# Weight sums for two projections: from accumulating DMAs to VectorE, in pieces, during the attention

## The chip, the core and the metric

The kernel runs on one core of a Trainium2 chip. Its time is the device time of one execution in microseconds; before the change the median of three runs is 1688.66 us (1685.91 to 1690.49). The core has TensorE (PE, matrix products), VectorE (DVE), ScalarE (ACT), GpSimd (POOL) and SyncE (SP). SyncE only issues transfers. GpSimd issues transfers too, among them the accumulating ones (the transfer adds to what stands at its destination). All transfers run on the same 16 DMA engines.

## What is computed

The reference is two layers of a decoder trunk on 512 positions of width 2048, all in float32. The even layer projects x into a gated short convolution and into a sparse attention of 8 heads, gates both, and projects back (`w_out`, 2048 x 2048). The odd layer is a gated MLP:

```python
def odd_layer(x, w_in, ln_g, ln_b, sgu_w, sgu_b, w_out):
    h = x @ w_in
    uv = jax.nn.gelu(h[..., :2 * D_SGU])
    z = h[..., 2 * D_SGU:]
    u, v = jnp.split(uv, 2, axis=-1)
    v = layer_norm(v, ln_g, ln_b)...
    mixed = jnp.einsum('gts,bnsgc->bntgc', w_causal, v) + sgu_b...
    y = u * mixed.reshape(bsz, s, D_SGU) * jax.nn.silu(z)
    return y @ w_out
```

After each layer stands a LayerNorm of the residual. The projections that matter here are those for u and z (2048 x 4096 together), for v, and the two output projections.

## The kernel before

A float32 operand is split into a high half (`hi`, rounded to float32r) and a low half (`lo`, the rest). ScalarE makes `hi` (L85), VectorE makes `lo` (L86), and every product is three matmuls. Weights come as raw pages of 128x1024 (512 KB) on SyncE's queue; there are four raw pages, and four pairs of `hi` and `lo` pages in the pool `wp`.

The stages follow each other: first the projections and the attention, head by head (the loop over h, six column units of 48 matmuls in each head and the head's scores, softmax and products); then five passes, each one Strassen-like product (`strassen`): the output projection of the even layer (wo0), v, u/z in two passes r = 0 and 1 (u and z share a pass: block column g of the pass belongs to half of u and z), and the last output projection (wo1). Strassen's scheme replaces eight block products by seven, numbered 1, 2, 5, 3, 6, 7, 4 in their order; each product p takes a block, or a sum of blocks, of the weights and of the activations. One product has two halves c of the inner dimension; for each half the activation piece is split (`shi`, `slo`) and then the weights of two block columns g are used by two row tiles m: 48 matmuls of 128x512 per (p, c), 14 of them per pass.

The sums of weight blocks come in two ways. In wo0, v and wo1 (`chained`, L613) pages x in SBUF are kept and GpSimd accumulates the next block into them; only sum 7 is made ahead, in DRAM. In the u/z passes (`plain`) all four sums 5, 7, 6, 4 are made ahead in DRAM by `weight_sums`. One step of it is four tiles of 512 KB: GpSimd writes one element of `after` into each tile (L227; this only makes the step wait for `after`), copies a block or an earlier sum into it (L232) and accumulates a second block (L238). There are 8 steps for each r and 2 for each of the three other sums. `early`, 16 steps, runs in the attention, two per head: wo0's, v's, all of r = 0 and the first four of r = 1. `late`, the other four of r = 1, and `steps1` (wo1's two) run in the passes: two steps of `late` in v (L817, L822), two in u/z r = 0, `steps1` in u/z r = 1 (L945, L949). A pass loads the ready sums as raw pages (L585).

In the u/z passes SyncE's queue also carries the rows of the LayerNorm (L874) and a residual chain: load `xs` (L898), two VectorE operations (L899, L900), store to `xres` (L901), with two buffers.

Engines run their instructions in a fixed order each. The framework that builds the program puts them in that order: what is ready first by its own estimate goes first, and among the ready ones the earlier in the text. Waits are semaphores; an engine whose next instruction waits does nothing else.

Of the kernel before, what the change touches and what calls it, by code (L numbers as in the profile page):

```python
# [65 lines left out]
def trunk(ctx, tc, xT, xn, oneh, cst, table, wa, wv, convw, posT, cw1, cw2, wo0, wuz, wv1, odg, odb, sguw, sgub, wo1, out):  # L66
# [24 lines left out]
    def load_unit(src, n, cut=1024):  # L91

        parts = []
        for c in range(0, n, cut):
            w = min(cut, n - c)
            raw = raw_page()
            nc.sync.dma_start(raw[:, :w], src[:, c:c + w])
            hi = wp.tile([P, 1024], F32R, tag="hi", name="whi", bufs=4)
            lo = wp.tile([P, 1024], F32R, tag="lo", name="wlo", bufs=4)
            split(hi[:, :w], lo[:, :w], raw[:, :w])  # L100
            parts.append((hi, lo))
        return parts
# [38 lines left out]
    for half in range(2):  # L141
        ws = {}
        for u in range(2):
            ws[u] = (wp.tile([P, 1024], F32R, tag="hi", name="whi", bufs=4), wp.tile([P, 1024], F32R, tag="lo", name="wlo", bufs=4))
        for i, (k0, k1) in enumerate(XCH[half]):
            for u, w0, w1 in WCH[half][i]:
                nc.sync.dma_start(wraw[u][half][:, w0:w1], wa[u][:, half * 1024 + w0:half * 1024 + w1])
            nc.sync.dma_start(xraw[:, k0:k1, :], xT[:, k0:k1, :])
        for i, (k0, k1) in enumerate(XCH[half]):
            for u, w0, w1 in WCH[half][i]:  # L150
                split(ws[u][0][:, w0:w1], ws[u][1][:, w0:w1], wraw[u][half][:, w0:w1])
            split(act_hi[:, k0:k1, :], act_lo[:, k0:k1, :], xraw[:, k0:k1, :])
        for k0, k1 in XCH[half]:
            for u in range(2):
                hi, lo = ws[u]
                for kt in range(k0, k1):
# [85 lines left out]
    sums0, steps0 = weight_sums(blocks(wo0), (7,), "ts0_")  # L242
    sumsv, stepsv = weight_sums(blocks(wv1), (7,), "tsv_")
    sums1, steps1 = weight_sums(blocks(wo1), (7,), "ts1_")
    sumsu, stepsu = zip(*(weight_sums(uz_blocks(r), (5, 7, 6, 4), f"tu{r}_") for r in range(2)))
    early = steps0 + stepsv + stepsu[0] + stepsu[1][:4]
    late = stepsu[1][4:]


    with ExitStack() as es:  # L250
# [229 lines left out]
        for h in range(NH):  # L480
            bh = ap.tile([P, BW], F32, name="bh")
            skew = rscr[h].rearrange("p r -> (p r)")[P - 1:P - 1 + P * (RLEN - 1)].rearrange("(p r) -> p r", r=RLEN - 1)[:, 0:BW]
            nc.sync.dma_start(bh, skew)
            bc = ap.tile([P, NT, NCMP], F32, name="bc")
            nc.gpsimd.memset(bc, NEG)
            for qb in range(NT):
                n = 8 * qb + 7
                j0 = BW - P + CB - 1 - P * qb
                nc.gpsimd.tensor_copy(bc[:, qb, :n], bh[:, j0:j0 + CS * (n - 1) + 1:CS])
            ps = next_a()  # L490
            qT = ap.tile([P, S], F32, name="qT", bufs=1)
            nc.scalar.activation(qT, ps, AF.Copy, scale=QSCALE)  # L492
            q_hi = ap.tile([P, S], F32R, name="q_hi", bufs=1)
            q_lo = ap.tile([P, S], F32R, name="q_lo", bufs=1)
            split(q_hi, q_lo, qT)
            q = qT, q_hi, q_lo
            if h == 0:
                cmp_half(1, 1)
                cmp_hidden(1)
            ps = next_a()  # L500
            if h == 0:
                cmp_out(1)
            bz = silu2(ps, "bz")
            for copies, _ in early[2 * h:2 * h + 2]:
                copies(qT[0:1, 0:1])
            t0, tc_ = softmax_branch(h, 0, q, bh, bc)
            compressed(h, tc_)

            ps = next_a()
            ah = ap.tile([P, S], F32, name="ah", bufs=1)  # L510
            nc.scalar.copy(ah, ps)
            transpose_c(tc_)
            p0 = transpose_p(t0)
            for _, adds in early[2 * h:2 * h + 2]:
                adds()
            ps = next_a()
            t1, _ = softmax_branch(h, 1, q, bh)
            u = ap.tile([P, S + 2], F32, name="u", bufs=1)
            nc.vector.memset(u[:, 0:2], 0.0)
            nc.vector.tensor_tensor(u[:, 2:], ps, ah, ALU.mult)  # L520
            nc.vector.tensor_scalar(ah, u[:, 0:S], convT[:, h, 0:1], None, ALU.mult)
            for k in (1, 2):
                nc.vector.scalar_tensor_tensor(ah, u[:, k:k + S], convT[:, h, k:k + 1], ah, ALU.mult, ALU.add)
            po = bank("po")
            products3(po, vc_hi[:, h // HPG], vc_lo[:, h // HPG], pc_hi, pc_lo, True, False)
            values_product(po, 0, p0)
            ps = next_a()
            nc.vector.tensor_tensor(ah, ps, ah, ALU.mult)
            p1 = transpose_p(t1)
            ps = next_a()  # L530
            az = silu2(ps, "az")
            nc.vector.scalar_tensor_tensor(y_sb[:, h, :], ah, YSCALE, az, ALU.mult, ALU.mult)  # L532
            values_product(po, 1, p1)
            nc.vector.scalar_tensor_tensor(y_sb[:, 8 + h, :], bz, YSCALE, po, ALU.mult, ALU.mult)
            if h == HPG - 1:
                key_unit(0)
                key_unit(1)
                values_and_gates(1)
                compressed_keys(1)
# [48 lines left out]
    def plain(get, sums):  # L588

        def unit(p, g, c, d):  # L590
            return raw_load(sums[p, g, c, d] if p in (5, 7, 6, 4) else get(*{1: (0, 0), 2: (1, 0), 3: (1, 1)}[p], g, c, d))
        return unit

    def chained(get, sums, pool, direct):
# [19 lines left out]
            return x[g, c, d]  # L614
        return unit

    def strassen(sp, src, unit, done, more=2, by_tile=False, wx=None, cuts=False):

# [15 lines left out]
        def weights(p, g, c):  # L634
            parts = []
            for d in range(2):
                raw = unit(p, g, c, d)
                pool = wx if wx and count[0] % 3 == 2 else wp
                count[0] += 1
                hi = pool.tile([P, 1024], F32R, tag="hi", name="whi", bufs=2 if pool is wx else 4)  # L640
                lo = pool.tile([P, 1024], F32R, tag="lo", name="wlo", bufs=2 if pool is wx else 4)
                split(hi, lo, raw)
                parts.append((hi, lo))
            return parts
# [107 lines left out]
    ex_ = ExitStack()  # L752
    ex = ex_.enter_context(tc.tile_pool(name="ex", bufs=1, side="right"))
    exq = ex.tile([P, 3, 2, 4, 256], F32, name="exq")
    xc_ = ExitStack()
    xc = xc_.enter_context(tc.tile_pool(name="xc", bufs=1))
    xhat = [dram.tile([P, DM], F32, name=f"xhat{m}") for m in range(NT)]
# [37 lines left out]
        if p == 5:  # L795
            nc.sync.dma_start(xv[:, 2 + m, cols(g, 0)], xn[(2 + m) * P:(3 + m) * P, cols(g, 0)])

    strassen(sp, in_place(quarters(y_sb)), chained(blocks(wo0), sums0, xc, (0,)), prefill)


    uv = {}
# [1 line left out]
    def done_v(p, g, m, b):  # L803
# [11 lines left out]
        elif p == 5:  # L815
            nc.scalar.copy(v(1, 1), b)
            if m:  # L817
                late[g][0](v(1, 1)[0:1, 0:1])
        elif p == 3:
            nc.scalar.copy(v(0, 1), b)  # L820
            if m:
                late[g][1]()  # L822
        elif p == 6:
            add(uv[g, m], b)

# [25 lines left out]
        return {1: xq(0, 0, c), 2: xq(0, 1, c), 5: xq(1, 0, c), 3: sd(c), 7: s3(c), 6: z(c), 4: xq(1, 1, c)}[p]  # L851

    made = []
    strassen(sp, x_sums, chained(blocks(wv1), sumsv, xc, (0,)), done_v)
    drain(len(later))
    mom = [moments(statsv, m, EPS) for m in range(NT)]
    xc_.close()
# [5 lines left out]
    with tc.tile_pool(name="sgu", bufs=2) as sg:  # L863
# [48 lines left out]
        def uz_done(r):  # L912
# [24 lines left out]
            def done(p, g, m, b):  # L937
# [3 lines left out]
                elif p == 2:  # L941
                    u[0, g, m] = tile()
                    nc.scalar.activation(u[0, g, m], b, AF.Gelu_apprx_tanh)
                    if m:
                        (late[2:], steps1)[r][g][0](u[0, g, m][0:1, 0:1])  # L945
                    if r == 1 and (g, m) == (1, 1):
                        later.extend(lambda mt=mt, q=q: y_turn(mt, q) for q in range(2) for mt in range(NT))
                elif p == 5:
                    if m:  # L949
                        (late[2:], steps1)[r][g][1]()  # L950
                    z[1, g, m] = tile()
                    nc.scalar.copy(z[1, g, m], b)
                elif p == 3:
# [20 lines left out]
        for r in range(2):  # L974
            for q in (2 * r, 2 * r + 1):
                values(q)
            for q in (2 * r, 2 * r + 1):
                residual_rows(q)
            strassen(sp, x_sums, plain(uz_blocks(r), sumsu[r]), uz_done(r), cuts=True)
        while later:  # L980
            drain(1)
    ex_.close()


    with tc.tile_pool(name="fin", bufs=1) as fin, tc.tile_pool(name="wx", bufs=1, side="right") as wx:
# [35 lines left out]
        strassen(sp, in_place(yT), chained(blocks(wo1), sums1, fin, (0,)), take1, by_tile=True, wx=wx)  # L1021


# [84 lines left out]
```

## Time and profile before

| | |
|---|---|
| median of 3 runs | 1688.66 us (1685.91 to 1690.49) |
| profiled execution | 1688.4 us, span 1686.6 us |
| mean granted TensorE clock | 0.973 |
| busy: TensorE, VectorE, ScalarE, GpSimd | 1597.9, 968.0, 685.8, 315.1 us |
| attention (with the first projections) | up to about 777 us |
| wo0, v | about 777 to 935, 935 to 1100 us |
| u/z r = 0, r = 1 | about 1100 to 1298, 1298 to 1485 us |
| wo1 and the end | about 1485 to 1687 us |

Times in the trace count from the start of the span. "Busy" is the time in which an engine executes; the granted clock is the share of TensorE's full clock (1 is 2.4 GHz). The time to landing of a transfer runs from its issue to its last byte.

### The profile page before, as it was taken

The page shows a single profiled execution, that of the slowest core. Times are in us where ns is not written, and L with a number is a line of the kernel's source. Part 1 is how long each engine was busy: PE and PEld are TensorE (multiplying, and loading weights), DVE is VectorE, ACT ScalarE, POOL GpSimd, SP SyncE. Part 2 cuts the span into 40 slices and gives each one's busy share as a digit, 9 for nine tenths or more (in the row PEclk, how much of TensorE's full clock was granted, in tenths as well). Part 3 has the DMA queues.
Part 4 walks back from the last instruction along what each step waited for, and adds up shares of the span by engine and source line. Part 5 has one row for each costly group of instructions (what it writes and reads, how often), then busy time and mean ns, then how long its engine had stood idle before and what let it go on. Part 6 is the DMA issues. An engine that isn't in the chain of part 4 may idle for free.

```text
span 1686.6 us, 19659 instructions
## 1 busy us (share of the span) xinstructions
PE 1597.9 (95%) x7333; PEld 1321.9 (78%) x7333; DVE 968.0 (57%) x1438; ACT 685.8 (41%) x965; POOL 315.1 (19%) x429
## 2 busy tenths in 40 slices
PE   8899999999999999999899999997699998999995
PEld 6698888888888888887688888775477886877784
DVE  5224453534244444455559875885389744974688
ACT  4123232323233323234355765552344554555441
POOL 0104041312021404041131214103100040011311
PEclk9899999999999999999999999998899999999898
DMA  5549696969259688699999979959966799579962
GB/s 208 195 138 258 147 237 145 248 165 236 84 175 219 187 182 215 149 248 251 225 226 241 276 194 273 246 176 292 259 212 197 241 277 250 170 241 280 225 158 81
DMA packets 157243, 355.34 MB, mean 211 GB/s; under 512 B 15227, under 2 KB 85683, under 8 KB 155868
## 3 DMA queue, kind: packets, MB, share of 16 engines
q0 software_dynamic: 72896, 139.00, 40.3%
q1 hardware_dynamic: 84108, 214.68, 38.3%
q8 instruction: 57, 0.93, 0.2%
q10 hardware_dynamic: 144, 0.41, 0.1%
q14 instruction: 38, 0.31, 0.1%
HBM read 341.42 MB, written 107.52 MB: 266 GB/s over the span
## 4 chain that ended last, share of the span: by engine, by line
PE 74%; DMA 13%; DVE 6%; issue 5%; ACT 1%; POOL 1%; SPq 0%; DVEq 0%; POOLq 0%; ACTq 0%
PE ps L111 12%; PE ps L113 12%; PE ps L112 12%; PE ps L664 9%; PE ps L665 9%; PE ps L663 9%; DMA raw<-in_wuz_dram 3%; DVE wlo L86 2%; DMA x<-in_wo_dram 2%; DMA row<-odrow 2%; PE ps_t L436 1%; DMA xs<-xhat 1%; DMA xv<-xres 1%; PE ps L122 1%; PE ps L120 1%
## 5 line engine op out<-in xcount | busy, mean ns | idle before, releaser
L86 DVE TENSOR_TENSOR wlo<-raw,whi 128x1024 fp32r<-128x1024 f32 (+2 forms) x322 | 385.3, 1203 | 452.8 <-ACT whi L85 447.4
L85 ACT CAST whi<-raw 128x1024 fp32r<-128x1024 f32 (+2 forms) x322 | 333.5, 1036 | 756.2 <-PE ps L112 312.6
L664 PE MATMUL ps<-wlo,shi 128*128 128x512 f32 x1120 | 450.6, 402 | 40.0 <-DVE wlo L86 39.8
L663 PE MATMUL ps<-whi,shi 128*128 128x512 f32 x1120 | 448.8, 404 | 16.2 <-ACT whi L85 15.5
L665 PE MATMUL ps<-whi,slo 128*128 128x512 f32 x1120 | 447.1, 400 | 1.3 <-DVE slo L86 1.3
L111 PE MATMUL ps<-act_hi,whi 128*128 128x512 f32 x864 | 340.4, 394 | 4.0 <-ACT whi L85 4.0
L113 PE MATMUL ps<-act_hi,wlo 128*128 128x512 f32 x864 | 337.6, 391 | 0.0
L112 PE MATMUL ps<-act_lo,whi 128*128 128x512 f32 x864 | 337.4, 390 | 0.0
L664 PEld LDWEIGHTS ps<-wlo,shi 128*128 128x128 f32 x1120 | 216.9, 194 | 96.4 <-DVE wlo L86 51.0
L663 PEld LDWEIGHTS ps<-whi,shi 128*128 128x128 f32 x1120 | 216.6, 193 | 67.9 <-ACT whi L85 20.5
L665 PEld LDWEIGHTS ps<-whi,slo 128*128 128x128 f32 x1120 | 216.4, 193 | 47.8 <-DVE slo L86 2.0
L111 PEld LDWEIGHTS ps<-act_hi,whi 128*128 128x128 f32 x864 | 163.0, 189 | 36.8 <-ACT whi L85 4.3
L113 PEld LDWEIGHTS ps<-act_hi,wlo 128*128 128x128 f32 x864 | 162.7, 188 | 35.0 <-DVE wlo L86 0.8
L112 PEld LDWEIGHTS ps<-act_lo,whi 128*128 128x128 f32 x864 | 162.9, 189 | 32.4
L86 DVE TENSOR_TENSOR wlo<-x,whi 128x1024 fp32r<-128x1024 f32 x84 | 101.7, 1219 | 40.9 <-ACT whi L85 40.3
L85 ACT CAST whi<-x 128x1024 fp32r<-128x1024 f32 x84 | 87.9, 1050 | 72.8 <-PE ps L665 61.7
L613 POOL DMA_DIRECT2D x<-in_wo_dram x48 | 42.6, 943 | 252.3 <-DMA x<-in_wo_dram 166.5
L238 POOL DMA_DIRECT2D tu<-in_wuz_dram x64 | 76.9, 2142 | 19.0 <-DMA tu<-tu 13.3
L227 POOL DMA_DIRECT2D tu<-qT x48 | 26.1, 603 | 251.7 <-ACT qT L492 251.7
L86 DVE TENSOR_TENSOR slo<-y_sb,shi 128x1024 fp32r<-128x1024 f32 x52 | 63.3, 1217 | 0.2 <-ACT shi L85 0.2
L85 ACT CAST shi<-y_sb 128x1024 fp32r<-128x1024 f32 x52 | 54.6, 1051 | 3.9 <-DVE y_sb L532 1.7
L417 ACT ACTIVATE t_sc<-t_sc,mx 128x128 f32<-128x128 f32 (+1 forms) x64 | 35.2, 551 | 17.2 <-DVE mx L414 17.1
(212 smaller groups left out, 1454.9 us busy)
## 6 DMA issues: line engine op xcount, KB each, us to landing
raw<-in_wa_dram SPq DMA_DIRECT2D x110, 512.0 KB, 5.4
tu<-in_wuz_dram POOLq DMA_DIRECT2D x96, 512.0 KB, 17.4
raw<-tu SPq DMA_DIRECT2D x64, 512.0 KB, 4.5
x<-in_wo_dram POOLq DMA_DIRECT2D x48, 512.0 KB, 10.0
raw<-in_wuz_dram SPq DMA_DIRECT2D x48, 512.0 KB, 5.7
raw<-in_wo_dram SPq DMA_DIRECT2D x40, 512.0 KB, 8.0
ts<-in_wo_dram POOLq DMA_DIRECT2D x32, 512.0 KB, 12.4
tu<-tu POOLq DMA_DIRECT2D x32, 512.0 KB, 8.4
```

Of the source, the lines that this page charges most:

```text
L85: nc.scalar.copy(hi, src)
L86: nc.vector.tensor_tensor(lo, src, hi.bitcast(F32), ALU.subtract)
L111: nc.tensor.matmul(ps, hi[:, w], act_hi[:, kt, :], start=kt == 0, stop=False)
L112: nc.tensor.matmul(ps, hi[:, w], act_lo[:, kt, :], start=False, stop=False)
L113: nc.tensor.matmul(ps, lo[:, w], act_hi[:, kt, :], start=False, stop=kt == KT - 1)
L227: nc.gpsimd.dma_start(h[0:1, 0:1], after)
L238: nc.gpsimd.dma_start(same(t[q, g, c, d], src), src, accum_op=ALU.add, max_dma_last_dim=1024)
L417: nc.scalar.activation(t[:, offs[qb]:offs[qb] + nk], t[:, offs[qb]:offs[qb] + nk], AF.Exp, bias=mx[:, qb:qb + 1], accum_out=sm[:, qb:qb + 1])
L613: nc.gpsimd.dma_start(x[g, c, d], get(*{5: (0, 1), 6: (1, 1), 4: (1, 0)}[p], g, c, d), accum_op=ALU.add)
L663: nc.tensor.matmul(o, s[0][:, k, ms], moving(hi, k), start=new and c == 0 and k == 0, stop=False, **kw)
L664: nc.tensor.matmul(o, s[0][:, k, ms], moving(lo, k), start=False, stop=False, **kw)
L665: nc.tensor.matmul(o, s[1][:, k, ms], moving(hi, k), start=False, stop=c == 1 and k == 3, **kw)
```

## The change

The four sums of the u/z weights are no longer made by accumulating DMAs. An item (r, g, c, i) loads four tiles of 128x512 (256 KB each, in runs of 2 KB) on SyncE's queue, adds four times on VectorE, in place, and stores each of the four as one sum on GpSimd's queue (runs of 1 KB). The tiles have four buffers in the attention's pool (`wsum`). There are 32 items, four per head, in the text at four places of the head loop. `early` keeps four steps, one for each of the first four heads. `steps1` moves into the v pass, to the place of the two steps of `late`; no step is left in the u/z passes.

The four buffers take the space of one `hi`/`lo` pair: `wp` has three pairs instead of four. The passes get the missing one from a pool `wx`: 3 + 1 pairs in wo0, v and u/z, 3 + 3 (before 4 + 2) in wo1, taken in turn.

```diff
-            hi = wp.tile([P, 1024], F32R, tag="hi", name="whi", bufs=4)
-            lo = wp.tile([P, 1024], F32R, tag="lo", name="wlo", bufs=4)
+            hi = wp.tile([P, 1024], F32R, tag="hi", name="whi", bufs=3)
+            lo = wp.tile([P, 1024], F32R, tag="lo", name="wlo", bufs=3)
...
-    sumsu, stepsu = zip(*(weight_sums(uz_blocks(r), (5, 7, 6, 4), f"tu{r}_") for r in range(2)))
-    early = steps0 + stepsv + stepsu[0] + stepsu[1][:4]
-    late = stepsu[1][4:]
+    early = steps0 + stepsv
+    sumsu = [{(q, g, c): dram.tile([P, 2, 4, 256], F32, name=f"tu{r}_{q}{g}{c}") for q in (5, 7, 6, 4) for g, c in GCS} for r in range(2)]
+
+    def uz_sums(pool, r, g, c, i):
+
+        q = 2 * r + g
+
+        def load(k, n):
+            t = pool.tile([P, 512], F32, tag="wsum", name="wsum", bufs=4)
+            nc.sync.dma_start(t, wuz[8 * q + 2 * i + n][:, (2 * k + c) * 512:(2 * k + c + 1) * 512])
+            return t
+
+        def add_store(p, t, o):
+            nc.vector.tensor_tensor(t, t, o, ALU.add)
+            nc.gpsimd.dma_start(sumsu[r][p, g, c][:, :, i], t.rearrange("p (d e) -> p d e", d=2))
+        b12, b22, b11, b21 = load(0, 1), load(1, 1), load(0, 0), load(1, 0)
+        add_store(7, b22, b12)
+        add_store(5, b12, b11)
+        add_store(6, b11, b22)
+        add_store(4, b21, b11)
+
+    uz_items = iter([(r, g, c, i) for r in range(2) for g, c in GCS for i in range(4)])
...
-            for copies, _ in early[2 * h:2 * h + 2]:
+            for copies, _ in early[h:h + 1]:
                 copies(qT[0:1, 0:1])
             t0, tc_ = softmax_branch(h, 0, q, bh, bc)
             compressed(h, tc_)
+            uz_sums(ap, *next(uz_items))
...
-            return raw_load(sums[p, g, c, d] if p in (5, 7, 6, 4) else get(*{1: (0, 0), 2: (1, 0), 3: (1, 1)}[p], g, c, d))
+            return raw_load(sums[p, g, c][:, d] if p in (5, 7, 6, 4) else get(*{1: (0, 0), 2: (1, 0), 3: (1, 1)}[p], g, c, d))
...
-                pool = wx if wx and count[0] % 3 == 2 else wp
+                pool, bufs = (wx, nx) if count[0] % (3 + nx) >= 3 else (wp, 3)
...
             if m:
-                late[g][0](v(1, 1)[0:1, 0:1])
+                steps1[g][0](v(1, 1)[0:1, 0:1])
...
-                    if m:
-                        (late[2:], steps1)[r][g][0](u[0, g, m][0:1, 0:1])
...
-                    if m:
-                        (late[2:], steps1)[r][g][1]()
```

## Rows read from the trace of the kernel before

**Rows 1.** Page, busy microseconds (share of the span), instructions.
```profile
PE 1597.9 (95%) x7333; PEld 1321.9 (78%) x7333; DVE 968.0 (57%) x1438; ACT 685.8 (41%) x965; POOL 315.1 (19%) x429
```

**Rows 2.** Busy time by stretch: engines, then granted clock, DMA share, GB/s.
```profile
60.00:777.00 717.00, 715.53 (x3576) 610.57 (x3577) 300.14 (x652) 218.54 (x423) 161.19 (x238) 1.00 0.75 193
1100.00:1298.00 198.00, 168.30 (x669) 132.24 (x668) 140.75 (x171) 84.61 (x97) 19.90 (x26) 0.91 0.79 229
1298.00:1485.00 187.00, 180.21 (x798) 147.41 (x797) 124.38 (x140) 97.77 (x116) 18.56 (x24) 0.98 0.80 235
```

**Rows 3.** TensorE's waits, 60 to 777 us: total, times, longest us.
```profile
PE ps L111 <- ACT whi L85: 4.0, 1, 4.0
...
```

**Rows 4.** TensorE's waits, 1100 to 1298 us.
```profile
PE ps L664 <- DVE wlo L86: 21.3, 9, 6.7
PE ps L663 <- ACT whi L85: 8.1, 5, 2.8
```

**Rows 5.** ScalarE in order of time, casts of activation pieces in the u/z passes.
```profile
1099.90 1.06 ACT L85 CAST shi<-y_sb 128x1024 fp32r<-128x1024 f32 x1
...
1163.30 1.04 ACT L85 CAST shi<-y_sb 128x1024 fp32r<-128x1024 f32 x1
...
1239.53 1.06 ACT L85 CAST shi<-exq 128x1024 fp32r<-128x1024 f32 x1
...
1302.72 1.06 ACT L85 CAST shi<-y_sb 128x1024 fp32r<-128x1024 f32 x1
...
1360.60 1.06 ACT L85 CAST shi<-y_sb 128x1024 fp32r<-128x1024 f32 x1
```

**Rows 6.** Chain that ended last, 1300 to 1330 us: start, us, what.
```profile
1308.35 1.73 PE pm L929 x8
...
```

**Rows 7.** GpSimd in order of time, u/z r = 0: first and last lines of 24 transfers.
```profile
1153.46 2.17 POOL L227 DMA_DIRECT2D tu<-uz  x4 [35.15 <-ACT uz L943]
...
1187.86 1.14 POOL L238 DMA_DIRECT2D tu<-in_wuz_dram  x1 [0.28 <-DMA tu<-tu]
```

**Rows 8.** Transfers issued from 1160 to 1225 us: count, KB, median us to landing.
```profile
raw<-in_wuz_dram SPq DMA_DIRECT2D x8, 512.0 KB, 14.7
raw<-tu SPq DMA_DIRECT2D x5, 512.0 KB, 13.6
```

**Rows 9.** Transfers issued from 1230 to 1290 us.
```profile
raw<-tu SPq DMA_DIRECT2D x19, 512.0 KB, 4.5
...
```

**Rows 10.** Busy time by stretch in u/z r = 1, columns as in rows 2.
```profile
1390.00:1420.00 30.00, 23.21 (x81) 16.86 (x80) 11.83 (x11) 12.87 (x17) 0.00 (x0) 0.89 1.15 263
1420.00:1450.00 30.00, 30.00 (x136) 24.88 (x135) 25.11 (x33) 16.25 (x18) 0.00 (x0) 1.00 0.53 169
```

**Rows 11.** Transfers of the whole program: count, KB, median us to landing.
```profile
xs<-xhat SPq DMA_DIRECT2D x16, 256.0 KB, 5.7
xres<-xs SPq DMA_DIRECT2D x16, 256.0 KB, 4.3
```

**Rows 12.** Groups by form: busy us, mean ns, idle before, what ended it.
```profile
L899 DVE TENSOR_TENSOR xs<-xs,row 128x512 f32<-128x512 f32 x16 | 10.8, 688 | 23.2 <-DMA xs<-xhat 18.3 <-DMA row<-in_odg_dram 3.3 <-issue 1.6
```

**Rows 13.** VectorE in order of time: start, us, instruction, idle before and its releaser.
```profile
1.05 0.06 DVE L550 MEMSET epst<- 128x1 f32 x1
...
838.95 0.69 DVE L705 BATCH_NORM_STATS2 stats<-xv 128x6 f32<-128x512 f32 x1 [5.57 <-DMA xv<-in_xn_dram]
...
1158.64 0.69 DVE L899 TENSOR_TENSOR xs<-xs,row 128x512 f32<-128x512 f32 x1 [3.41 <-DMA xs<-xhat]
...
1258.69 0.69 DVE L899 TENSOR_TENSOR xs<-xs,row 128x512 f32<-128x512 f32 x1 [2.38 <-DMA xs<-xhat]
...
1336.78 0.69 DVE L899 TENSOR_TENSOR xs<-xs,row 128x512 f32<-128x512 f32 x1 [1.17 <-DMA xs<-xhat]
```

**Rows 14.** ScalarE in order of time, casts of two weight pieces in the attention.
```profile
485.41 1.05 ACT L85 CAST whi<-raw 128x1024 fp32r<-128x1024 f32 x1 [4.39 <-PE ps L112]
...
490.80 1.05 ACT L85 CAST whi<-raw 128x1024 fp32r<-128x1024 f32 x1 [3.20 <-PE ps L112]
```

More of the change, by code (lines that the diff above doesn't have):

```diff
@@ L143, in trunk @@
         for u in range(2):
-            ws[u] = (wp.tile([P, 1024], F32R, tag="hi", name="whi", bufs=4), wp.tile([P, 1024], F32R, tag="lo", name="wlo", bufs=4))
+            ws[u] = (wp.tile([P, 1024], F32R, tag="hi", name="whi", bufs=3), wp.tile([P, 1024], F32R, tag="lo", name="wlo", bufs=3))
         for i, (k0, k1) in enumerate(XCH[half]):
@@ L513, in trunk @@
             p0 = transpose_p(t0)
-            for _, adds in early[2 * h:2 * h + 2]:
+            for _, adds in early[h:h + 1]:
                 adds()
+            uz_sums(ap, *next(uz_items))
             ps = next_a()
@@ L523, in trunk @@
                 nc.vector.scalar_tensor_tensor(ah, u[:, k:k + S], convT[:, h, k:k + 1], ah, ALU.mult, ALU.add)
+            uz_sums(ap, *next(uz_items))
             po = bank("po")
@@ L532, in trunk @@
             nc.vector.scalar_tensor_tensor(y_sb[:, h, :], ah, YSCALE, az, ALU.mult, ALU.mult)
+            uz_sums(ap, *next(uz_items))
             values_product(po, 1, p1)
@@ L615, in chained, with strassen @@
         return unit
-    def strassen(sp, src, unit, done, more=2, by_tile=False, wx=None, cuts=False):
+    def strassen(sp, src, unit, done, wx, nx, more=2, by_tile=False, cuts=False):
         count = [0]
@@ L637, in weights @@
                 raw = unit(p, g, c, d)
-                pool = wx if wx and count[0] % 3 == 2 else wp
+                pool, bufs = (wx, nx) if count[0] % (3 + nx) >= 3 else (wp, 3)
                 count[0] += 1
-                hi = pool.tile([P, 1024], F32R, tag="hi", name="whi", bufs=2 if pool is wx else 4)
-                lo = pool.tile([P, 1024], F32R, tag="lo", name="wlo", bufs=2 if pool is wx else 4)
+                hi = pool.tile([P, 1024], F32R, tag="hi", name="whi", bufs=bufs)
+                lo = pool.tile([P, 1024], F32R, tag="lo", name="wlo", bufs=bufs)
                 split(hi, lo, raw)
@@ L754, in trunk @@
     exq = ex.tile([P, 3, 2, 4, 256], F32, name="exq")
+    wx_ = ExitStack()
+    wx = wx_.enter_context(tc.tile_pool(name="wx", bufs=1))
     xc_ = ExitStack()
@@ L796, in prefill @@
             nc.sync.dma_start(xv[:, 2 + m, cols(g, 0)], xn[(2 + m) * P:(3 + m) * P, cols(g, 0)])
-    strassen(sp, in_place(quarters(y_sb)), chained(blocks(wo0), sums0, xc, (0,)), prefill)
+    strassen(sp, in_place(quarters(y_sb)), chained(blocks(wo0), sums0, xc, (0,)), prefill, wx, 1)
     uv = {}
@@ L821, in done_v @@
             if m:
-                late[g][1]()
+                steps1[g][1]()
         elif p == 6:
@@ L853, in trunk @@
     made = []
-    strassen(sp, x_sums, chained(blocks(wv1), sumsv, xc, (0,)), done_v)
+    strassen(sp, x_sums, chained(blocks(wv1), sumsv, xc, (0,)), done_v, wx, 1)
     drain(len(later))
@@ L978, in trunk @@
                 residual_rows(q)
-            strassen(sp, x_sums, plain(uz_blocks(r), sumsu[r]), uz_done(r), cuts=True)
+            strassen(sp, x_sums, plain(uz_blocks(r), sumsu[r]), uz_done(r), wx, 1, cuts=True)
         while later:
@@ L982, in trunk @@
     ex_.close()
+    wx_.close()
     with tc.tile_pool(name="fin", bufs=1) as fin, tc.tile_pool(name="wx", bufs=1, side="right") as wx:
@@ L1019, in take1 @@
                     nc.sync.dma_start(gb[:, i], odg[i:i + 1].to_broadcast([P, DM]))
-        strassen(sp, in_place(yT), chained(blocks(wo1), sums1, fin, (0,)), take1, by_tile=True, wx=wx)
+        strassen(sp, in_place(yT), chained(blocks(wo1), sums1, fin, (0,)), take1, wx, 3, by_tile=True)
 def t5_bucket(n):
```

## The prediction, on record before the result

> **What bounds the kernel now.** I read the busy shares first, then the stages, then in the stages the waits of the tensor engine, then the engine that it waits for. The whole program is bound by TensorE: 95% of the span [rows 1]. But the stages differ [rows 2]. During the attention (60 to 777 us) TensorE is busy for 715.5 of 717 us at full clock, and its only wait over 1 us is one of 4.0 us near its start [rows 3]. Nothing done there can win time; something done there can lose it. The two passes for u and z (I call them uz0 and uz1) are different: uz0 is busy for 168.3 of 198 us at a mean clock of 0.91, uz1 for 180.2 of 187 us. What ends the idle time in uz0 is the weight pages: 21.3 us on the low half (VectorE's subtraction), 8.1 us on the high half (ScalarE's cast) [rows 4].
>
> The pace tells what this costs. Each pass has 14 (product, half) steps, and each starts with one cast of an activation piece on ScalarE. Undisturbed, the casts are 10.88 us apart: in uz1 from 1302.72 to 1360.60 there are five steps in 57.9 us, which is 5 x 10.88 plus 3.5 us of 16 small "pm" matmuls (two groups of 1.73) [rows 5, 6]. In uz0 the four steps from 1163.30 to 1239.53 take 76.2 us instead of 43.5: 32.7 us lost in one place. The five before (1099.90 to 1163.30) lose 63.4 - 54.4 = 9.0.
>
> What happens there: GpSimd issues two steps of the u/z weight sums, 16 transfers of 512 KB, from 1153 to 1189 us [rows 7]. Between 1160 and 1225 SyncE's weight pages land after 14.7 and 13.6 us; from 1230 on, with GpSimd's queue empty, after 4.5 us [rows 8, 9]. In uz1 the two steps of the out-projection's sums (16 transfers again) do the same on a smaller scale: from 1390 to 1420 TensorE gets 81 matmuls done, where the next 30 us hold 136 [rows 10]. 55 x 0.227 us (10.88 / 48) is 12.5 us; a few records can be missing, so I take 11.
>
> **The change, part by part.**
>
> *Sums out of uz0 and uz1.* The last two u/z steps leave uz0; the two steps of the out-projection move from uz1 to the V pass, into the place that two other u/z steps leave there (16 transfers for 16): V counts as 0. uz0: of the 9.0 us before 1163, only the last ten microseconds lie behind the first transfer at 1153; I give the sums 1.3 and leave 7.7 to VectorE, which works off the V pass there. Gain 32.7 + 1.3 = 34. uz1: 11. That the next limit lies far off is read from uz1 before 1360: with the same loads, rows and residual work and no sums it loses nothing. Bounds: 33 to 44 for uz0 (all its loss), 8 to 13 for uz1.
>
> *32 items on VectorE.* Each item loads four tiles of 256 KB, adds four times and stores four tiles. An add of 128x512 takes 688 ns [rows 12], so 128 x 0.688 = 88 us more on an engine that is busy for 300 of the attention's 717 us. As work it fits: 0. GpSimd is busy for 0.54 (2.17 / 4) to 1.14 us per transfer [rows 7]; 128 stores at that are 69 to 146 us, where it is busy for 161 now [rows 2] and loses 48 copies and 48 accumulations. SyncE, which does nothing but issue, gets 128 loads more. Price of the issuing: 0.
>
> *The wait that it adds.* VectorE runs its instructions in a fixed order. Behind an add that waits for its load stand the next low halves of the weights, and TensorE waits for those. The order is fixed ahead of the run and by readiness, not by the text: a memset that the text has after the attention runs at 1.05 us [rows 13]. So I expect the items to run back to back from the first free moment, held back only by their four buffers: load, add, store, next load. If the store and load take longer on the chip than the order assumed, every item holds VectorE by the difference. Cover: a weight piece lasts 5.4 us on TensorE [rows 14]; with three page pairs instead of four the split is 2 x 5.44 - 1.05 - 1.22 = 8.6 us ahead (14.0 before). The nearest row to such an item is the residual chain in the uz passes (load xs, two VectorE operations, store, next load, two buffers). Its 16 loads made VectorE wait 18.3 us, 1.14 us each [rows 12], and at worst, outside the congested stretch, 3.41 [rows 13]. But most of those waits fall where VectorE was behind its order; of the last eight loads, from 1247 us on, two were waited for, 2.38 and 1.17 us [rows 13]: 0.44 each. Low end: 0 (below it only if the lighter GpSimd queue helped, and there is no idle time to win). High end: 32 x 3.41 - 8.6 = 100 us. Nearest: 32 x 0.44 - 8.6 = 5.5 us. To this I add some 5 us for the start, where the stage's one 4.0 us wait shows weights only just in time and 2 MB per item would now share the DMA engines. I take 10.
>
> *Three page pairs in the attention, 3 + 1 afterwards, 3 + 3 in the last projection.* Afterwards the number of pages is as before: 0. In the attention the shorter cover costs only together with a wait of VectorE: within the 10.
>
> Rule and row: the attention has no stall while VectorE serves only operands that engines make; where it serves operands that a DMA brings, it does stall: at 838.95 us a statistics operation waited 5.57 us for an accumulating DMA [rows 13], and the next low half came late. The Trainium skill (Perfetto Trace Analysis, Tensor Engine Instruction) says that VectorE, ScalarE and GpSimd take their instructions strictly in order. By that rule the adds turn each late load into a late weight page, and the change may be slower; the trace agrees with it, and it is the first rival below.
>
> A price: the residual chain's loads land after 5.7 us and its stores after 4.3 [rows 11]. The Trainium skill (DMA: Bandwidth & Descriptors, Anatomy of one DMA) fits a DMA as about 2.0 us plus its bytes over 436 GB/s, 2.6 us for 256 KB, an estimate by that page. By it an item's chain would be some 5 us shorter than by the rows and the charge of 10 would go to 0 (1643 us); the rows hold.
>
> **Sum.** Against the profiled execution's 1688.4 us (span 1686.6; the median of the runs, 1688.66, is the same): 1688.4 - 34 - 11 + 10 = 1653.
>
> **The rivals.**
>
> 1. *The items hold up VectorE during the attention.* One mechanism: each item's load comes later than the fixed order assumed, and the lag adds up, since the next item can't start before the store has landed. Place: the attention, from its first microseconds until the 32nd item. For: the residual chain's waits of 1.14 to 3.41 us, the cut from 14.0 to 8.6 us of cover, GpSimd's own sums for the first four heads in the same queue as the stores. Against: in undisturbed stretches the mean is 0.44. It decides the sign above (45 + 8.6) / 32 = 1.7 us per item. At 2.3 (between 1.14 and 3.41): 32 x 2.3 - 8.6 = 65, 1643 + 65 = 1708 us.
>
> 2. *uz0's stall is SyncE's order, not the sums.* SyncE also carries the rows and the residual chain, whose stores wait for VectorE, and the weight pages stand behind them. Then uz0 keeps most of its loss and only 11 + 10 come back: 1688.4 - 21 + 10 = 1677. For: the chain of waits in uz0 passes through row and xs loads. Against: uz1 before 1360 has the same and loses nothing.
>
> 3. *The traffic has only moved.* 64 MB of loads and stores in 1 and 2 KB runs come into a stage whose DMA share is 0.75 already [rows 2]; weight pages there land as late as in uz0, and the attention loses the 45 us that the passes gain: 1688, no change. Against: the attention carried 96 transfers of 512 KB for the same sums, and lost nothing by them.
>
> **How the numbers follow.** Forecast (gain of 45, little lost: 1637 to 1670) 0.58; rival 2 and in-between cases (1670 to 1683) 0.12; rival 3 0.07; rival 1 0.23. So faster 0.70, within 0.3% 0.07, slower 0.23; 0.3%, 5 us, is about what a measurement of this kernel tells from no change. The forecast's own range is 1637 to 1670: all of uz0's and uz1's loss and no charge is 1688.4 - 44 - 13 = 1631, of which I leave 6 us out. For 8 in 10 the range goes up into rival 1: 1637 to 1702.
>
> **What would show it.** Right: uz0's 14 steps 10.9 us apart from 1160 on, weight pages landing after about 5 us, uz0 near 165 us, no GpSimd transfers in either pass; the attention still about 717 us with VectorE near 390. Wrong: in the attention, idle TensorE ahead of matmuls that wait for the low halves, and VectorE idle until a "wsum" load lands, item after item (rival 1); uz0 still slow with GpSimd's queue empty (rival 2); weight pages of the attention landing after 10 us and more (rival 3). A VectorE that waits over 1.7 us per item makes the prediction wrong in sign.

## The result, and the profile after

The changed kernel takes 1752.96 us (median of 4 runs, 1752.0 to 1757.77), the kernel before in the same job 1687.38: a ratio of 1.0392 (95% interval 1.0366 to 1.0417). It is 66 us slower where I forecast 35 us faster.

The first casts of the passes (ScalarE in order of time, as in [rows 5]: start, us, instruction) give the stages. Of the kernel before, those that [rows 5] doesn't show (wo0, v, wo1), then of the kernel after:

```profile
777.44 1.04 ACT L85 CAST shi<-y_sb 128x1024 fp32r<-128x1024 f32 x1
...
935.46 1.05 ACT L85 CAST shi<-y_sb 128x1024 fp32r<-128x1024 f32 x1
...
1479.64 1.06 ACT L85 CAST shi<-y_sb 128x1024 fp32r<-128x1024 f32 x1
```

```profile
881.91 1.04 ACT L85 CAST shi<-y_sb 128x1024 fp32r<-128x1024 f32 x1
...
1206.44 1.06 ACT L85 CAST shi<-y_sb 128x1024 fp32r<-128x1024 f32 x1
...
1379.47 1.06 ACT L85 CAST shi<-y_sb 128x1024 fp32r<-128x1024 f32 x1
...
1544.39 1.06 ACT L85 CAST shi<-y_sb 128x1024 fp32r<-128x1024 f32 x1
```

| stage, us | before | after | difference |
|---|---|---|---|
| up to the end of the attention | 777.4 | 881.9 | +104.5 |
| wo0 | 158.0 | 160.2 | +2.2 |
| v | 164.4 | 164.3 | -0.1 |
| u/z r = 0 | 202.8 | 173.0 | -29.8 |
| u/z r = 1 | 176.9 | 164.9 | -12.0 |
| wo1 and the end | 207.0 | 205.8 | -1.2 |

The v pass of the kernel after starts at 1042.14, and the last row reaches to the end of the span (1686.6 and 1750.2). So the passes gave back nearly what was forecast, and the attention lost more than twice that. Where in the attention, the windows tell (columns as in [rows 2]). The kernel before, then the kernel after:

```profile
60.00:480.00 420.00, 418.53 (x2171) 360.63 (x2172) 168.57 (x354) 124.21 (x240) 85.25 (x132) 0.99 0.72 188
```

```profile
60.00:480.00 420.00, 349.78 (x1605) 290.63 (x1606) 198.15 (x383) 91.26 (x175) 119.97 (x189) 0.89 0.85 262
480.00:882.00 402.00, 402.00 (x1980) 341.96 (x1979) 174.90 (x390) 125.56 (x249) 10.00 (x23) 1.00 0.32 98
```

All of the loss lies before 480 us, and there the items end: the last store is issued at 475.0 us (below). From 480 us on TensorE is never idle and its clock is full. Before it, TensorE is idle for 70.2 us instead of 1.5, and the granted clock is 0.89 instead of 0.99 (a mean over stretches at 2.4 and at 1.2 GHz). By these means 349.8 us of work cost 349.8 x (1 - 0.89 / 0.99) = 35 us more, an estimate. With the 68.7 us of idle time that is 104.

What the instructions of an item do, by the view of the tile "wsum" (line, engine, operation, count: ns at least, median and at most, first and last start):

```profile
L254 SPq DMA_DIRECT2D wsum<-in_wuz_dram x128: 327/328/1067, 28.0 to 470.2; - x128
L258 DVE TENSOR_TENSOR wsum<-wsum x128: 618/692/697, 36.7 to 473.3; 128x512 f32<-128x512 f32 x128
L259 POOL DMA_DIRECT2D tu<-wsum x128: 625/672/2121, 37.7 to 475.0; - x128
```

The page on the same (busy us, mean ns, idle time before and what ended most of it; then KB and us to landing):

```profile
L258 DVE TENSOR_TENSOR wsum<-wsum 128x512 f32<-128x512 f32 x128 | 88.4, 691 | 186.8 <-DMA wsum<-in_wuz_dram 181.1
...
wsum<-in_wuz_dram SPq DMA_DIRECT2D x128, 256.0 KB, 3.9
tu<-wsum POOLq DMA_DIRECT2D x128, 256.0 KB, 4.0
```

The adds take 88.4 us of VectorE, as forecast. But VectorE stood idle for 181.1 us until loads landed, 5.7 us per item; 1.7 was the point at which the sign turns. The waits of SyncE's queue from 20 to 600 us (who waits for what: us in total, times, longest) show the other side:

```profile
SPq L254 <- DMA tu<-wsum: 276.9, 95, 20.0
```

Loads of the next item wait for stores of the last one, 277 us in total, and SyncE's queue holds the weight pages too. One turn of this ring stands in the chain that ended last (start, us, what):

```profile
118.69 0.67 POOL tu L259
...
119.41 3.98 DMA tu<-wsum
...
123.44 0.33 SPq L254
...
123.86 4.66 DMA raw<-in_wa_dram
128.52 0.71 DVE wlo L86
...
129.28 0.59 PE ps L121
```

A store lands; only then can SyncE issue the load that waits for its buffer; behind that load stands a weight page; its split and the matmuls follow. What TensorE waited for, from 60 to 600 us:

```profile
PE ps L113 <- DVE wlo L86: 13.1, 6, 3.4
PE ps_s L398 <- DVE p_lo L86: 12.5, 1, 12.5
PE ps L353 <- DVE rep L351: 10.9, 2, 10.4
PE ps_t L455 <- DVE t_sc L442: 10.4, 4, 4.5
```

What VectorE makes comes late, and not the low halves of weights alone: the low halves of probabilities (`p_lo`), the scaled softmax (`t_sc`) and copied values (`rep`) too.

### The profile page after: what moved, and what is told of

Same layout as the page of the kernel before. It is cut to its first block, busy times and chain, and to the rows that moved or that the text cites. A ratio compares the mean times of both kernels' runs of the same rounds, so it can differ in the third digit from the quotient of the medians.

```text
span 1750.2 us, 20093 instructions
## 1 busy us (share of the span) xinstructions
PE 1618.9 (92%) x7333; PEld 1336.0 (76%) x7333; DVE 1048.8 (60%) x1566; ACT 684.7 (39%) x965; POOL 256.4 (15%) x365
## 4 chain that ended last, share of the span: by engine, by line
PE 56%; DMA 16%; issue 15%; DVE 6%; POOL 4%; ACT 1%; SPq 1%; POOLq 0%; DVEq 0%; ACTq 0%
PE ps L687 10%; PE ps L688 10%; PE ps L686 10%; PE ps L113 6%; PE ps L111 6%; PE ps L112 6%; POOL tu L259 3%; DVE wlo L86 2%; DMA tu<-wsum 2%; DMA x<-in_wo_dram 2%; DMA ts<-in_wo_dram 2%; DMA wsum<-in_wuz_dram 1%; DMA raw<-in_wa_dram 1%; DMA bh<-rscr 1%; DMA xs<-xhat 1%
## 5 line engine op out<-in xcount | busy, mean ns | idle before, releaser
L687 PE MATMUL ps<-wlo,shi 128*128 128x512 f32 x1120 | 445.2, 398 | 23.3 <-DVE wlo L86 22.9
L686 PE MATMUL ps<-whi,shi 128*128 128x512 f32 x1120 | 443.6, 399 | 6.7 <-ACT whi L85 6.1
L688 PE MATMUL ps<-whi,slo 128*128 128x512 f32 x1120 | 441.6, 395 | 1.3 <-DVE slo L86 1.3
L113 PE MATMUL ps<-act_hi,wlo 128*128 128x512 f32 x864 | 343.4, 397 | 13.2 <-DVE wlo L86 13.1
L111 PE MATMUL ps<-act_hi,whi 128*128 128x512 f32 x864 | 346.2, 401 | 5.2 <-ACT whi L85 5.2
L112 PE MATMUL ps<-act_lo,whi 128*128 128x512 f32 x864 | 342.4, 396 | 0.0
L258 DVE TENSOR_TENSOR wsum<-wsum 128x512 f32<-128x512 f32 x128 | 88.4, 691 | 186.8 <-DMA wsum<-in_wuz_dram 181.1
L111 PEld LDWEIGHTS ps<-act_hi,whi 128*128 128x128 f32 x864 | 166.7, 193 | 38.8 <-ACT whi L85 5.5
L259 POOL DMA_DIRECT2D tu<-wsum x128 | 89.3, 761 | 281.7 <-DVE wsum L258 202.8
L85 ACT CAST whi<-x 128x1024 fp32r<-128x1024 f32 x84 | 88.0, 1051 | 70.2 <-PE ps L688 59.7
```

The source lines that it names most:

```text
L85: nc.scalar.copy(hi, src)
L111: nc.tensor.matmul(ps, hi[:, w], act_hi[:, kt, :], start=kt == 0, stop=False)
L112: nc.tensor.matmul(ps, hi[:, w], act_lo[:, kt, :], start=False, stop=False)
L113: nc.tensor.matmul(ps, lo[:, w], act_hi[:, kt, :], start=False, stop=kt == KT - 1)
L258: nc.vector.tensor_tensor(t, t, o, ALU.add)
L259: nc.gpsimd.dma_start(sumsu[r][p, g, c][:, :, i], t.rearrange("p (d e) -> p d e", d=2))
```

## The experiments

The theory I took to the chip: VectorE is held by adds whose loads come late (rival 1). Its rivals: the traffic (rival 3), the three page pairs, and the 88 us of adds as work. no_items, no_adds, no_adds_pool, half and no_stores leave out work, so their values are not the reference's. Diffs are against the changed kernel unless said.

**no_items.** The floor: no items at any of the four places, and the passes load a plain block where a sum was.

```diff
-            uz_sums(ap, *next(uz_items))
...
-            return raw_load(sums[p, g, c][:, d] if p in (5, 7, 6, 4) else get(*{1: (0, 0), 2: (1, 0), 3: (1, 1)}[p], g, c, d))
+            return raw_load(get(*{1: (0, 0), 2: (1, 0), 3: (1, 1), 5: (0, 1), 7: (1, 1), 6: (0, 0), 4: (1, 0)}[p], g, c, d))
```

> The changed kernel without the items: no loads, adds and stores in the attention; the passes for u and z load plain weight blocks where the sums would stand (so their values are not the reference's). Three page pairs in the attention stay. All theories but C: the attention at its old 777 us and the passes as after the change, 1687 - 42 = 1645. Rival C (three page pairs cost the attention its time): the attention stays above 800 us, 1670 to 1750.

1649.8 us, ratio 0.9782 (0.9758 to 0.9806); the attention ends at 778.87. I call these two figures the floor. The whole loss hangs on the items, and without them the other parts of the change win 2.2%.

**pages3.** The kernel before with three page pairs and the pool `wx`, nothing else.

```diff
-            hi = wp.tile([P, 1024], F32R, tag="hi", name="whi", bufs=4)
+            hi = wp.tile([P, 1024], F32R, tag="hi", name="whi", bufs=3)
```

> The kernel before with the changed page pairs alone (3 in the attention, 3 + 1 and 3 + 3 in the passes), its sums made by accumulating DMAs as before. Theory: 1687, within 5 us. Rival C: slower, 1700 to 1750.

1687.53 us, ratio 1.0006 (0.9992 to 1.0021). The shorter cover costs nothing by itself.

**no_adds.** Loads and stores stay, VectorE takes no part.

```diff
         def add_store(p, t, o):
-            nc.vector.tensor_tensor(t, t, o, ALU.add)
```

> The changed kernel without the adds: the items load four tiles and store them as they are (the sums are left out), back to back as before, 64 MB in the attention. VectorE has neither the work nor the wait. Theory: the attention near 780 us, 1645 to 1660. Rival A (work on VectorE): the same 1645 to 1660, so this run doesn't tell it from the theory. Rival B (the traffic): the attention stays above 850 us, 1720 or more.

1753.78 us, ratio 1.0402 (1.0384 to 1.042): as slow as with the adds. My theory fell here, since it named VectorE alone. SyncE in order of time shows what holds the weights now (one load of `raw` is one weight page):

```profile
224.94 2.21 SPq L254 DMA_DIRECT2D wsum<-in_wuz_dram  x4
227.20 0.42 SPq L97 DMA_DIRECT2D raw<-in_wa_dram  x1
234.65 2.29 SPq L254 DMA_DIRECT2D wsum<-in_wuz_dram  x4
236.99 0.42 SPq L97 DMA_DIRECT2D raw<-in_wa_dram  x1
```

From one page to the next it is 9.8 us, where TensorE uses one up in 5.4 [rows 14]. Between them stands one turn of the loop (load, store, next load). The waits of SyncE (20 to 700 us) and of ScalarE (20 to 900 us):

```profile
SPq L254 <- DMA tu<-wsum: 255.9, 105, 23.8
```

```profile
ACT whi L85 <- DMA raw<-in_wa_dram: 247.4, 29, 33.1
```

In no_items ScalarE waits 38.1 us for those pages. So the loop makes the whole loss without VectorE, through SyncE's queue and GpSimd's, which carries the stores.

**gated.** Each item's adds get an operand (a column of ones) made from a value of the head (`bz`, then `ah`, `u` and `az` at the other places), so that the fixed order can't put them earlier.

```diff
-            nc.vector.tensor_tensor(t, t, o, ALU.add)
+            nc.vector.scalar_tensor_tensor(t, t, one, o, ALU.mult, ALU.add)
...
+        one = pool.tile([P, 1], F32, tag="one", name="one")
+        nc.vector.tensor_scalar(one, after, 0.0, 1.0, ALU.mult, ALU.add)
...
-            uz_sums(ap, *next(uz_items))
+            uz_sums(ap, bz[:, 0:1], *next(uz_items))
```

> The changed kernel with one difference: each item's four adds also need a value that the head makes (a column of bz, ah, u or az times 0 plus 1), so that the fixed order puts them at four places of each head instead of one item after another. The work, the loads, the stores and the buffers are the same; an add becomes a scalar_tensor_tensor. Theory (the items run back to back, and VectorE stands still for each late load, the lag adding up): the loads have mostly landed when the adds come up, the attention takes under 795 us instead of 882, and the time is 1645 to 1665. Rival A (88 us more work on VectorE): the attention stays long, 1730 or more. Rival B (the traffic of the items): the same, 1730 or more. Rival C (three page pairs instead of four): 1700 or more.

1663.47 us, ratio 0.9871 (0.9849 to 0.9893). Same loads, sums and stores, 90 us less than the changed kernel; they are also spread out (loads from 26.8 to 777.0 us instead of 28.0 to 470.2), so this run alone doesn't tell the order from the density of the traffic. The attention ends at 791.45, 12.6 us over the floor: VectorE still waits 49.0 us for loads up to 700 us, and the last item's adds run to 801 us, into wo0, whose start waits 8.0 us for a high half.

**no_adds_pool.** As no_adds, and the loads go to GpSimd's queue: the same traffic, no link of the loop on SyncE or VectorE.

```diff
-            nc.sync.dma_start(t, wuz[8 * q + 2 * i + n][:, (2 * k + c) * 512:(2 * k + c + 1) * 512])
+            nc.gpsimd.dma_start(t, wuz[8 * q + 2 * i + n][:, (2 * k + c) * 512:(2 * k + c + 1) * 512])
```

> As no_adds (items load and store, back to back, no adds; the sums are left out), but the loads are issued on GpSimd's queue like the stores, so neither SyncE nor VectorE has an instruction of the loop in its order. The same 64 MB in the attention. Theory 2 (the loop of store and next load holds whichever in-order queue carries a part of it, and SyncE's weight pages stand behind it): the attention near 780 us, 1645 to 1660. Rival B (the traffic itself): still 1720 or more.

1695.2 us, ratio 1.0065 (1.005 to 1.008). The traffic is as dense as in no_adds (285 GB/s from 60 to 402 us against 280 from 60 to 393), and 59 of no_adds' 104 us over the floor are gone, so traffic isn't the main cause. But 45 remain, which I had not expected. TensorE's largest waits and the one of ScalarE behind the second:

```profile
PE hp L332 <- DMA raw<-in_cw_dram: 18.2, 2, 9.9
PE ps_s L416 <- ACT qT L510: 15.5, 1, 15.5
```

```profile
ACT qT L510 <- DMA ts<-qT: 24.9, 1, 24.9
```

ScalarE can't overwrite `qT` before GpSimd's one-element transfer that reads it (the L227 of `early`) is done, and that stands behind the loop in GpSimd's queue. The loads for `hp` wait 24.3 us in SyncE's queue for the transfer `rrow`, which GpSimd issues from a raw page behind the loop.

**loads_pool.** The changed kernel with its loads on GpSimd's queue (the same edit, the adds kept); SyncE is out of the loop.

> The changed kernel with the items' loads on GpSimd's queue; the adds stay on VectorE, back to back. Theory 2: SyncE is free, VectorE still stands in the loop, so the attention stays long: 1715 to 1760. If only SyncE's queue matters: 1645 to 1665. Rival B: 1720 or more.

1788.34 us, ratio 1.0616 (1.0598 to 1.0635), 28 us above the range I expected; VectorE waits 203.3 us for loads. 139 us over the floor, of which no_adds_pool has 45: the other 94 come with the adds. Over 70 us of TensorE's waits from 60 to 930 us end with something that VectorE makes. One engine out of the loop is no cure.

**all_pool.** Loads, adds and stores on GpSimd; no other engine in the loop.

```diff
-            nc.sync.dma_start(t, wuz[8 * q + 2 * i + n][:, (2 * k + c) * 512:(2 * k + c + 1) * 512])
+            nc.gpsimd.dma_start(t, wuz[8 * q + 2 * i + n][:, (2 * k + c) * 512:(2 * k + c + 1) * 512])
...
-            nc.vector.tensor_tensor(t, t, o, ALU.add)
+            nc.gpsimd.tensor_tensor(t, t, o, ALU.add)
```

> The changed kernel with loads, adds and stores of the items all on GpSimd, back to back, the results as the reference's. Theory 2: no queue that TensorE depends on carries the loop, the attention near 780 us, 1645 to 1665; the adds are slower on GpSimd, which matters only if the items then last beyond the attention. Rival B: 1720 or more. If GpSimd's adds slow VectorE by sharing its way to SBUF, between 1665 and 1700.

1751.13 us, ratio 1.04 (1.0369 to 1.0431), a miss by 86 us and more. The waits, and the add as GpSimd does it:

```profile
PE ps_s L417 <- ACT qT L511: 71.0, 2, 49.4
```

```profile
ACT qT L511 <- DMA tsv<-qT: 58.7, 1, 58.7
```

```profile
L258 POOL TENSOR_TENSOR wsum<-wsum x128: 1254/1388/2110, 9.7 to 579.3; 128x512 f32<-128x512 f32 x128
```

The loop is longer (an add takes 1.39 us instead of 0.69), and the one-element transfers that read `qT` stand behind it.

**half.** Sixteen items, two per head; the second u/z pass loads plain blocks where sums were, as in no_items.

```diff
-            uz_sums(ap, *next(uz_items))
...
-            return raw_load(sums[p, g, c][:, d] if p in (5, 7, 6, 4) else get(...))
+            return raw_load(sums[p, g, c][:, d] if p in (5, 7, 6, 4) and r == 0 else get(...))
```

> The changed kernel with half of its items (16, for the first u/z pass; the second pass loads plain blocks where its sums would stand). Theory 2 (the lag adds up item by item): about half of the attention's loss of 104 us, 1647 + 52 = 1700, within 12. A price paid once (start, first items): 1740 or more. Something that comes from the shorter page pool or the passes: 1750 as before.

1686.81 us, ratio 1.0012 (0.9997 to 1.0028), 1 us below the range I expected. 16 items cost 37 us over the floor, 32 cost 103: the lag grows with the items, and faster than their number.

**no_stores.** Loads and adds, no stores; the passes load plain blocks.

```diff
-            nc.gpsimd.dma_start(sumsu[r][p, g, c][:, :, i], ...)
```

> The changed kernel without the items' stores (and with plain blocks where the sums would stand in the passes): loads and adds back to back. The loop is load, add, next load. Theory 2: the part of the lag that comes from the stores goes; the waits of VectorE fall from 181 us to under half, and the time to 1660 to 1715. If the loads alone hold VectorE: 1730 or more.

1676.74 us, ratio 0.9931 (0.9909 to 0.9952): 27 over the floor. Without the store in the loop three quarters of the loss is gone, with every add and every load still there. The bytes per item are halved, but while the items run the transfers are no thinner: 272 GB/s, DMA share 0.86, against 262 and 0.85 in the changed kernel (the lines stand further down).

**all_pool_tiny.** As all_pool, with the one-element transfers reading a copy of `qT`'s element that VectorE makes.

```diff
-                copies(qT[0:1, 0:1])
+                tiny = ap.tile([1, 8], F32, name="tiny")
+                nc.vector.tensor_copy(tiny[0:1, 0:1], qT[0:1, 0:1])
+                copies(tiny[0:1, 0:1])
```

> As all_pool (items wholly on GpSimd, back to back), but the one-element transfers that mark the start of a step of the other sums read a tiny copy of q instead of q itself, so that ScalarE's next q no longer waits for GpSimd's queue. Theory 2 (what stands behind the loop in an in-order queue is what costs, there the release of q): the two waits of ScalarE for those transfers (31 and 59 us) go, the attention near 785 us, 1650 to 1670. If GpSimd's adds or the traffic cost the time: 1730 or more.

1696.17 us, ratio 1.0048 (1.0032 to 1.0064). The 55 us of `qT` are back, so that wait is shown as their cause; 46 over the floor remain, a miss again. The largest waits that are left are for things behind the loop in GpSimd's queue as well (`rrow` again, and the bias `bc`); that they make the 46 is argued from these waits, not tried:

```profile
PE hp L333 <- DMA raw<-in_cw_dram: 20.4, 2, 11.0
PE ps_ct L487 <- DVE t_c L483: 15.5, 2, 11.0
```

```profile
DVE t_c L426 <- POOL bc L508: 32.4, 2, 19.2
```

**gated2.** As gated, at other places (the diff is against gated): an item before the first head, then at `bz`, `u`, `ah` after the head's second product, and `az` (none at the end of the last head). All 32 items are still made.

```diff
+        uz_sums(ap, kcT[:, 0, 0:1], *next(uz_items))
...
-            uz_sums(ap, ah[:, 0:1], *next(uz_items))
...
             uz_sums(ap, u[:, 2:3], *next(uz_items))
+            uz_sums(ap, ah[:, 0:1], *next(uz_items))
...
+            if h < NH - 1:
+                uz_sums(ap, az[:, 0:1], *next(uz_items))
```

> As gated, with the places of the adds spread more evenly (bz, u, ah after its second product, az; no item at the end of the last head, one before the first head). Theory 2: every place is at least one loop (about 14 us) behind the one before, so the attention loses less than the 12.6 us that gated lost against no_items: 1650 to 1662. If the rest of gated's loss is VectorE's work or the traffic: 1663 as gated.

1649.31 us (1648.75 to 1650.26), ratio 0.9771 (0.9756 to 0.9785): the floor of no_items, with all sums made. It beats both kernels. The adds and the idle time before them by the view of the tile, then SyncE's waits from 20 to 780 us:

```profile
L258 DVE SCALAR_TENSOR_TENSOR wsum<-wsum,one x128: 734/747/754, 119.6 to 771.0; 128x512 f32<-128x512 f32 x128
...
  DMA wsum<-in_wuz_dram: 1.1, 2
```

```profile
SPq L254 <- DMA tu<-wsum: 243.8, 100, 16.9
```

128 adds of 747 ns, 96 us, are free now. An item comes every 21 us in the mean ((771.0 - 119.6) / 31), and VectorE waits 1.1 us in all for loads. SyncE waits nearly as long as in the changed kernel, but now with room to spare: TensorE is busy for 714.87 of the 718 us from 60 to 778.

## Why the prediction was wrong

**The passes: right.** Forecast gains of 34 and 11, measured 29.8 and 12.0. The weight pages of uz0 land after 4.9 and 5.1 us in the median (sums and blocks) instead of 13.6 and 14.7 [rows 8], as forecast. So rival 2 (SyncE's order in uz0) is out. TensorE still waits there for 9.9 us, 8.1 of them on low halves. The prediction had left 7.7 us to VectorE, so these waits explain about 2 of the 4 us that are short of 34; the rest isn't shown. The v pass at 0 was right; the three page pairs at 0 too (pages3).

**VectorE's work at 0: right.** It is 88.4 us in the changed kernel, and 96 us in gated2, where it costs nothing.

**The wait that it adds: this step failed.** It charged 10 us (32 x 0.44 less 8.6 of cover, and 5 for the start); the attention lost 104.5, 3.3 us per item, about the worst row of the residual chain (3.41) that gave the step's high end of 100. The nearest row was not near: the residual chain's loads come in pairs with other work between them (VectorE serves two around 1175 us and the next two at 1247), so that a late one can catch up. The step itself said that the items would run back to back, and then the lag adds up. The worst of that chain's waits, 9.08 us at 1174.68, was left out because it fell where GpSimd's accumulating transfers were under way; but four steps of such transfers stay in the attention.

How much it adds up can be read. TensorE has the same matmuls in every kernel (7333 on the pages of before and after), so its progress at any time is a number of matmuls. I count those from 60 us to the last load of each kernel (the first figure in brackets), and look in no_items, where TensorE runs nearly undisturbed, for when the same number is reached. The difference is the lag. The kernel after, at 242 and at 470 us; no_adds; half; no_stores:

```profile
60.00:242.00 182.00, 153.34 (x795) 132.27 (x796) 78.79 (x151) 39.26 (x77) 51.31 (x83) 0.89 0.88 278
60.00:470.00 410.00, 342.16 (x1576) 284.37 (x1576) 191.94 (x374) 90.26 (x174) 115.26 (x181) 0.89 0.85 262
```

```profile
60.00:393.00 333.00, 261.67 (x1218) 215.09 (x1219) 86.51 (x185) 63.90 (x124) 101.75 (x162) 0.87 0.88 280
```

```profile
60.00:242.00 182.00, 150.74 (x791) 129.33 (x792) 78.42 (x151) 39.22 (x77) 52.24 (x82) 0.91 0.87 277
```

```profile
60.00:293.00 233.00, 210.75 (x1095) 181.85 (x1095) 146.99 (x282) 60.78 (x120) 30.54 (x51) 0.93 0.86 272
```

And no_items:

```profile
60.00:205.00 145.00, 141.98 (x792) 124.42 (x793) 51.73 (x105) 40.08 (x77) 15.99 (x33) 0.98 0.57 175
60.00:269.00 209.00, 205.98 (x1096) 178.29 (x1097) 81.37 (x176) 61.21 (x120) 26.57 (x50) 0.98 0.57 168
60.00:296.00 236.00, 232.98 (x1218) 200.79 (x1219) 88.81 (x185) 68.09 (x128) 29.38 (x56) 0.99 0.54 161
60.00:371.50 311.50, 308.48 (x1575) 264.35 (x1576) 122.30 (x260) 91.63 (x174) 39.58 (x72) 0.99 0.54 156
```

| kernel | last load, us | same matmul in no_items | lag | attention over the floor |
|---|---|---|---|---|
| after | 470 | 371.5 | 98.5 | 103.0 |
| no_adds | 393 | 296 | 97 | 102.7 |
| half | 242 | 205 | 37 | 39.3 |
| no_stores | 293 | 269 | 24 | 24.4 |

The last column is the first cast of wo0 (881.91, 881.59, 818.17, 803.22) less 778.87. In each kernel the lag at the last load is the loss of the attention, within 6 us: it adds up while the items run, and nothing of it is caught up afterwards. Per item, the changed kernel has (371.5 - 28) / 32 = 10.7 us of undisturbed work and takes (470.2 - 28.0) / 32 = 13.8 on the chip. The difference of 3.1 is the lag divided by 32, a mean and not a second measurement. Without adds it is 8.4 against 11.4, without stores 7.5 against 8.3. What the framework reckoned for each transfer I didn't look at.

The mean hides that the items differ. At 242 us, after 16 items, the changed kernel has done 795 matmuls, about as many as no_items by 205 (792). So the first 16 items bring a lag of 37 us, 2.3 each, as half does with its 16; the other 16 bring 61, 3.8 each. One reason can be seen in the trace. GpSimd's queue also carries the accumulating steps that `early` keeps. Three of the four fall among the items, and an item's stores stand behind each. GpSimd, SyncE and VectorE at the second of these steps:

```profile
283.89 2.52 POOL L238 DMA_DIRECT2D ts<-in_wo_dram  x2 [0.31 <-issue]
285.51 3.91 POOL L259 DMA_DIRECT2D tu<-wsum  x4
...
300.17 0.97 SPq L254 DMA_DIRECT2D wsum<-in_wuz_dram  x2
...
304.88 0.69 DVE L258 TENSOR_TENSOR wsum<-wsum 128x512 f32<-128x512 f32 x1 [14.08 <-DMA wsum<-in_wuz_dram]
```

The stores issued from 268 to 300 us land after 14.7 us in the median, where 4.0 is the median of all; SyncE issues its next load only at 300.17, and VectorE stands for 14.08 us. From its first load to that of the next item this item takes 30 us, and those around the first and the third step take 30 and 34, where the median is 12. Counted as above, the lag grows by about 48 of its 98.5 us in the three stretches with such a step (158 to 200, 268 to 312, 370 to 425 us). The prediction had named this under rival 1 (GpSimd's own sums in the same queue as the stores) and gave it no price. No run leaves these steps out, so what they cost by themselves is not shown.

**The other queues: left out.** The prediction gave SyncE, "which does nothing but issue", a price of the issuing of 0, and looked for the waiting instruction on VectorE only. But SyncE issues in order too. Its load waits for a store, and a weight page behind it waits as well; no_adds shows that the loop makes the whole loss without VectorE. GpSimd's queue is a third: with the whole loop there (no_adds_pool, all_pool, all_pool_tiny) the attention is 45 to 103 us late. That the one-element transfers make 55 us of it in all_pool is shown by all_pool_tiny; the rest is argued from the waits.

The Trainium skill (Perfetto Trace Analysis, Tensor Engine Instruction) says that VectorE, ScalarE and GpSimd are strict FIFOs; the changed kernel agrees, where VectorE stands idle for 181.1 us ahead of adds. SyncE behaves in the same way in no_adds, with its 255.9 us of waits.

**The rivals.** Rival 1 was right in kind, place and condition, though it named VectorE alone, and was given 0.23. Its price, 65 us, came from 2.3 us per item, which is what the first 16 items cost; over all 32 it was 3.3. Rival 3 (traffic) is out as the main cause. Its sign was weight pages that land after 10 us and more; they land as before (issued from 60 to 480 us: count, KB, median us to landing; before, then after):

```profile
raw<-in_wa_dram SPq DMA_DIRECT2D x62, 512.0 KB, 5.3
raw<-in_wa_dram SPq DMA_DIRECT2D x50, 512.0 KB, 5.4
```

In gated2 they take 5.7 us, and nothing is lost. gated2 moves the same 64 MB through the attention, spread over 735 us of loads instead of 442; no_adds_pool and no_stores keep the traffic as dense and lose less than half as much as no_adds and the changed kernel. The lower clock is a consequence: from 60 to 480 us it is 0.89 with the loop, and in no_items, to 371.5 us, 0.99.

**Open.** How the changed kernel's loss divides between SyncE and VectorE: SyncE and GpSimd make as much without VectorE (no_adds), the adds bring 94 us without SyncE (loads_pool), and in one ring the three wait for each other. In no_stores the loop on SyncE is shorter too, since a load there waits for an add only, and GpSimd is out of it. What GpSimd's accumulating steps add is open as well.

## What to carry to other kernels

A piece of work that loads, computes, stores and loads again into the same buffers is a loop, and is to be priced as one: its turn on the chip (landing, compute, landing, over the buffers, and whatever else stands in the same queues in front of its stores) against the time that the fixed order leaves per turn, and the difference times the number of turns. It is charged to every in-order queue that carries a link, the queue that only issues transfers among them, since a wait there holds whatever stands behind it. Where the order puts such work by readiness, give it a real operand from the place where it should run: here that turned 4% slower into 2.3% faster (gated2), with the same sums and transfers.

## What the runs showed that I had not expected

- GpSimd adds 128x512 float32 in 1.39 us (spans on GpSimd are rough), VectorE in 0.69.
- A transfer of one element, behind a waiting loop in GpSimd's queue, held ScalarE for 58.7 us (all_pool).
- A load of 256 KB by SyncE landed after 3.9 us in the median, at most 14.8 for loads and stores together; the Trainium skill (DMA: Bandwidth & Descriptors, Anatomy of one DMA) has a fit for transfers that GpSimd issues, by which 256 KB would take 2.6 us, an estimate; those that GpSimd issues here, the stores, took 4.0 in the median.
